# Log-sum-exp of 16,384 rows: another split of the loads and rows between three engines, and another middle range check

## The chip, the core and the metric

The kernel runs on one core of a Trainium2 chip. The metric is the device time of one execution in microseconds (us); the median of three runs is given. The core's engines have separate instruction queues and meet only at semaphores: TensorE (PE), VectorE (DVE), ScalarE (ACT), GpSimd (POOL) and SyncE (SP), which here issues all loads and stores to one DMA queue that 16 DMA engines serve.

## The reference

```
x: (32, 512, 1024) float32
max_x = max(x, axis=-1)
out   = max_x + log(sum(exp(x - max_x), axis=-1))        # (32, 512) float32
```

Each of the 32 x 512 = 16,384 rows of 1024 numbers gives one number.

## The kernel before

The rows are spread over 128 partitions, 128 rows to each. The first 112 rows of a partition (W = 112) come from one part of x, the last 16 from another, so that the results can be stored in two pieces. From here on "a row" is one row of 1024 elements on every partition at once.

The kernel leaves out the subtraction of the maximum: it sums exp(x) directly and takes the logarithm. At the end a range check looks whether all sums lie between 1e-15 and 1e15; if one does not, a second, safe pass runs (everything under `nc.If`). With these inputs it is skipped.

The work is written out by hand in the table LOADS. Each entry is one DMA load: its size in rows and what is done with it. A load goes into `ring`, which holds 48 rows; a load that does not fit at the end starts again at the front. SP issues the loads in order, and each waits (function `load`) until the rows that it overwrites have been summed. For each part of an entry ACT computes one exponential over the part's rows in place (L213), and the letters say who sums them:

- R n: DVE sums n rows with one reduction (L224).
- G n: POOL adds the second half of each of n rows to the first (L219, "folds"), later DVE sums the halves with one reduction (`sum_folded`, L148). That sum comes at the end of the load's entry, or where H or C stands.
- T n: DVE takes n rows one by one by halves: one operation adds the halves and accumulates the sum (`add_halves`, L156); a small read of the accumulator follows each.
- a, b: the two pieces of the last row, 256 and 768 elements. DVE takes a by halves, ACT sums b while it exponentiates it (L208).
- C: the middle range check over the sums so far. L: the early Ln of the first 112 sums (L199), whose store (L245) follows.

Several letters joined by + share one exponential. A part's exponential may reach beyond its last row, to the end of the load; the rest of that row comes with the next load. So an engine's order is the order of the table, and what one engine has not finished can hold up the others only through the semaphores: ACT waits for landings, DVE and POOL for ACT, DVE for POOL, SP for the sums that free the ring.

The range check (`check`, L163 to L174) is, for a group of sums: one operation with two inputs that counts in `bad` the sums below 1e-15 (L163), a reduction that gives their `total` (L167), and two small matmuls that add both into `count`. It is called once at C and once at the end. After the last sum the end is: ACT's Ln of sums 112 to 126 (L249), which waits for DVE's last sum; the Ln of the last row (L251), whose two pieces meet there; the store (L255); beside it the second check, the comparison (L263) and the branch. Ahead of the sixteenth load's pieces `addr_align(128)` (L186) puts padding into DVE's instructions up to a boundary.

Of the kernel before, what the change touches and what calls it, by code (L numbers as in the profile page):

```python
# [9 lines left out]
LOW, HIGH = 1e-15, 1e15  # L10
# [7 lines left out]

LOADS = [
# [4 lines left out]
]  # L26


# [23 lines left out]
def kernel(  # L52
# [5 lines left out]
    nc = tc.nc  # L58
# [7 lines left out]
    AF = mybir.ActivationFunctionType  # L66
    AX = mybir.AxisListType
    ALU = mybir.AluOpType

    x_flat = x.flatten_outer_dims()  # L70
    n, d = x_flat.shape
    assert n % P == 0
    NC = n // P
    H = d // 2
    W = NC - B
    LAST = NC - 1
# [6 lines left out]
    def source(e0, size):  # L83
# [6 lines left out]
        ])  # L90
        for size, parts in LOADS
    ]
    assert sum(size for size, _ in loads) == NC * d

    def sbuf(name, cols, dtype=fp32, rows=P):
        return nc.alloc_sbuf_tensor(name, [rows, cols], dtype).ap()

    ring = sbuf("ring", RING * d)
    sumexp = sbuf("sumexp", NC + 1)
    res = sbuf("res", NC)  # L100
    clamped = sbuf("clamped", NC)
    bad = sbuf("bad", 2)
    total = sbuf("total", 2)
    far = sbuf("far", 1)
    ones = sbuf("ones", 1)
    fine = sbuf("fine", 1, i32, 1)
    count = nc.alloc_psum_tensor("count", [1, 1], fp32).ap()

    landed = [nc.alloc_semaphore(f"landed{i}") for i in range(len(loads))]
    act = Counted(nc, nc.scalar, "act")  # L110
    dve = Counted(nc, nc.vector, "dve")
    pe = Counted(nc, nc.tensor, "pe")
    pool = Counted(nc, nc.gpsimd, "pool")
# [8 lines left out]
    constants = pool.did(nc.gpsimd.memset(far, 100 * HIGH))  # L122


    users = []

    def load(i, here, done_before, size):
        for a, b, who, at in users:
            if a < here + size and b > here:
                sp.wait(who, at)  # L130
        users[:] = [u for u in users if not (u[0] < here + size and u[1] > here)]
        return nc.sync.dma_start(
            out=ring[:, here : here + size], in_=source(done_before, size)
        ).then_inc(landed[i], 16)

    c = 0
    p = 0
    here = 0
    done_before = 0
    first_load = None  # L140
    folded = []
    summed = []

    def sum_folded():
        for c0, p0, s, at in folded:
            dve.wait(pool, at)
            half = ring[:, p0 : p0 + s * d].rearrange("p (c d) -> p c d", d=d)[:, :, 0:H]
            at = dve.did(nc.vector.reduce_sum(out=sumexp[:, c0 : c0 + s], in_=half, axis=AX.X))  # L148
            users.append((p0, p0 + s * d, dve, at))
            summed.append((c0, c0 + s, at))  # L150
        folded.clear()

    def add_halves(v, col):
        h = v.shape[-1] // 2
        lo = v[:, 0:h]
        return dve.did(nc.vector.scalar_tensor_tensor(  # L156
            out=lo, in0=lo, scalar=1.0, in1=v[:, h : 2 * h],
            op0=ALU.mult, op1=ALU.add, accum_out=sumexp[:, col : col + 1],
        ))

    def check(k, c0, c1):
        dve.wait(dve, dve.n)
        dve.did(nc.vector.scalar_tensor_tensor(  # L163
            out=clamped[:, c0:c1], in0=sumexp[:, c0:c1], scalar=LOW, in1=sumexp[:, c0:c1],
            op0=ALU.max, op1=ALU.not_equal, accum_out=bad[:, k : k + 1],
        ))
        at = dve.did(nc.vector.reduce_sum(  # L167
            out=total[:, k : k + 1], in_=sumexp[:, c0:c1], axis=AX.X
        ))
        if k == 0:  # L170
            pe.wait(pool, constants)
        pe.wait(dve, at)
        pe.did(nc.tensor.matmul(count, lhsT=bad[:, k : k + 1], rhs=far, start=k == 0, stop=False))  # L173
        pe.did(nc.tensor.matmul(count, lhsT=ones, rhs=total[:, k : k + 1], start=False, stop=False))  # L174

    for i, (size, parts) in enumerate(loads):
        if here + size > RING * d:
            assert here == p
            p = here = 0
        dma = load(i, here, done_before, size)  # L180
        first_load = first_load or dma.ins
        end = here + size
        done_before += size
        act.wait(landed[i], 16)
        if i == ALIGNED:
            nc.vector.addr_align(128)  # L186
        for k, part in enumerate(parts):
            if part[0][0] == "H":
                sum_folded()
                continue  # L190
            if part[0][0] == "C":
                sum_folded()
                checked = c
                check(0, 0, c)
                continue
            if part[0][0] == "L":
                assert c >= W
                act.wait(dve, max(at for c0, _, at in summed if c0 < W))
                ln_early = act.did(nc.scalar.activation(  # L199
                    out=res[:, 0:W], in_=sumexp[:, 0:W], func=AF.Ln  # L200
                ))
                continue
            rows = sum(s for how, s in part if how in "RTG")
            more = any(q[0][0] not in "HLC" for q in parts[k + 1 :])
            upto = p + rows * d if more else end
            v = ring[:, here:upto]
            if part[-1][0] == "b":
                last = act.did(nc.scalar.activation(  # L208
                    out=v, in_=v, func=AF.Exp, accum_out=sumexp[:, NC : NC + 1]
                ))  # L210
                here = upto
                continue
            at = act.did(nc.scalar.activation(out=v, in_=v, func=AF.Exp))  # L213
            here = upto
            for how, s in part:
                rows = ring[:, p : p + s * d].rearrange("p (c d) -> p c d", d=d)
                if how == "G":
                    pool.wait(act, at)
                    folded.append((c, p, s, pool.did(nc.gpsimd.tensor_tensor(  # L219
                        out=rows[:, :, 0:H], in0=rows[:, :, 0:H], in1=rows[:, :, H:d], op=ALU.add,  # L220
                    ))))
                elif how == "R":
                    dve.wait(act, at)
                    users.append((p, p + s * d, dve, dve.did(nc.vector.reduce_sum(  # L224
                        out=sumexp[:, c : c + s], in_=rows, axis=AX.X
                    ))))
                    summed.append((c, c + s, dve.n))
                elif how == "T":
                    dve.wait(act, at)
                    for r in range(s):  # L230
                        n_sums = add_halves(rows[:, r, :], c + r)
                        users.append((p + r * d, p + (r + 1) * d, dve, n_sums))
                        summed.append((c + r, c + r + 1, n_sums))
                elif how == "a":
                    dve.wait(act, at)
                    summed.append((LAST, NC, add_halves(ring[:, p:upto], LAST)))
                    s = 0
                c += s
                p += s * d
        sum_folded()  # L240
        assert here == end
    assert c == LAST
    assert sorted(q for c0, c1, _ in summed for q in range(c0, c1)) == list(range(NC))
    sp.wait(act, ln_early)
    nc.sync.dma_start(out=out_rows, in_=res[:, 0:W]).then_inc(sp.sem, 16)  # L245

    sums = dve.n
# [1 line left out]
    act.did(nc.scalar.activation(out=res[:, W:LAST], in_=sumexp[:, W:LAST], func=AF.Ln))  # L249
    act.wait(act, last)  # L250
    ln_last = act.did(nc.scalar.activation(  # L251
        out=res[:, LAST:NC], in_=sumexp[:, NC : NC + 1], func=AF.Ln, bias=sumexp[:, LAST:NC]
    ))
    sp.wait(act, ln_last)
    nc.sync.dma_start(out=out_rest, in_=res[:, W:NC]).then_inc(stored, 16)  # L255

    check(1, checked, NC)
    pe.wait(act, last)
    at = pe.did(nc.tensor.matmul(  # L259
        count, lhsT=ones, rhs=sumexp[:, NC : NC + 1], start=False, stop=True  # L260
    ))
    dve.wait(pe, at)
    at = dve.did(nc.vector.tensor_scalar(out=fine, in0=count, scalar1=HIGH, scalar2=None, op0=ALU.is_lt))  # L263
# [6 lines left out]
    with nc.If(all_fine < 1):  # L270
# [5 lines left out]
        for c0 in range(0, NC, RING):  # L276
            s = min(RING, NC - c0)
            v = ring[:, 0 : s * d].rearrange("p (c d) -> p c d", d=d)
# [4 lines left out]
            for c1, c2 in ((c0, edge), (edge, c0 + s)):  # L283
                if c1 == c2:
                    continue
                nc.scalar.dma_start(
                    out=ring[:, (c1 - c0) * d : (c2 - c0) * d],
                    in_=source(c1 * d, (c2 - c1) * d),
# [4 lines left out]
                out=neg, in_=v, op=ALU.max, axis=AX.X, negate=True  # L293
# [3 lines left out]
                out=v, in0=v, in1=neg[:, :, None].to_broadcast([P, s, d])  # L297
# [5 lines left out]
                out=sumexp[:, c0 : c0 + s], in_=v, axis=AX.X  # L303
# [71 lines left out]
```

## Time and profile before

| | |
|---|---|
| median of three runs | 162.37 us (162.37 to 162.44) |
| the profiled execution, its own time | 162.29 us |
| its span | 161.0 us |
| DVE, ACT, POOL, PE busy | 119.1, 115.0, 32.4, 0.5 us |
| DMA queue of the loads, share of 16 engines | 97.4% |
| read from HBM | 67.11 MB |

The span runs from the program's first instruction (the first load, at 0.00) to the last. Times in the timeline are us from its start. A timeline line gives start, duration, engine, line of the kernel, operation, what it writes and reads, the shape, and in brackets the idle time before it with what ended that. Runs of the same operation are merged (x3). An instruction may start while the one before it on the same engine is still shown: its fixed part overlaps. The chain of waits goes back from the last instruction, at each step to what released it. Groups by form give busy us, the mean ns of one, and the idle time before.

### The profile page before, as it was taken

What the parts mean: (1) busy time and instruction counts of PE and PEld (TensorE: products, weight loads), DVE (VectorE), ACT (ScalarE), POOL (GpSimd) and SP (SyncE); (2) the same over time, 40 slices, a digit from 0 to 9 for tenths busy, and PEclk for the clock granted to TensorE, in tenths of its full rate; (3) what the DMA queues carried; (4) which work ended last, traced back from release to release, by engine and by line L of the source; (5) the groups of instructions that cost most, each with busy time, mean ns of one, the idle gap of its engine ahead of it and who ended that gap; (6) DMA issues with size and microseconds to landing.
All of it is one profiled execution on the core that took longest, in us unless ns stands there. A gap on an engine that the chain in (4) does not pass through costs nothing.

```text
span 161.0 us, 202 instructions
## 1 busy us (share of the span) xinstructions
PE 0.5 (0%) x10; PEld 0.3 (0%) x10; DVE 119.1 (74%) x48; ACT 115.0 (71%) x32; POOL 32.4 (20%) x15
## 2 busy tenths in 40 slices
PE   0000000000000000000000000000000000000000
PEld 0000000000000000000000000000000000000000
DVE  0000000019999499995999999999999999999996
ACT  3000059980799609994199938996997999799995
POOL 0000000000000000000008800006950806737700
DMA  7996996996996996996999969899997999999991
GB/s 261 521 521 261 521 521 261 521 521 261 521 521 261 521 521 261 521 521 261 495 469 469 469 294 507 378 401 469 455 455 336 448 420 450 390 435 412 425 409 33
DMA packets 2882, 67.18 MB, mean 417 GB/s; under 512 B 577, under 2 KB 577, under 8 KB 1345
## 3 DMA queue, kind: packets, MB, share of 16 engines
q1 hardware_dynamic: 2880, 67.18, 97.4%
q14 instruction: 2, 0.01, 0.0%
HBM read 67.11 MB, written 0.07 MB: 417 GB/s over the span
## 4 chain that ended last, share of the span: by engine, by line
DVE 52%; DMA 30%; ACT 12%; POOL 4%; issue 1%; DVEq 0%; PE 0%
DVE sumexp L224 38%; DMA ring<-in_x_dram 30%; ACT ring L213 12%; DVE sumexp L148 10%; POOL ring L219 4%; DVE ring L156 3%; DVE clamped L163 1%; DVEq L186 0%; DVE total L167 0%; PE count L173 0%; DVE fine L263 0%; PE count L259 0%; PE count L174 0%
## 5 line engine op out<-in xcount | busy, mean ns | idle before, releaser
L213 ACT ACTIVATE ring<-ring 128x16384 f32<-128x16384 f32 (+22 forms) x26 | 112.3, 4371 | 42.5 <-DMA ring<-in_x_dram 42.4
L224 DVE TENSOR_REDUCE sumexp<-ring 128x16 f32<-128x16384 f32 (+6 forms) x10 | 96.1, 9639 | 40.0 <-ACT ring L213 40.0
L219 POOL TENSOR_TENSOR ring<-ring 128x1024 f32<-128x1024 f32 (+5 forms) x9 | 32.1, 3579 | 118.3 <-ACT ring L213 118.3
L148 DVE TENSOR_REDUCE sumexp<-ring 128x2 f32<-128x1024 f32 (+5 forms) x9 | 16.1, 1802 | 0.4 <-POOL ring L219 0.4
L156 DVE SCALAR_TENSOR_TENSOR ring<-ring 128x512 f32<-128x512 f32 (+1 forms) x11 | 6.5, 642 | 0.0
L120 ACT ACT_TABLE_LOAD x1 | 1.3, 1283 | 1.4 <-PEq L61 1.4
L163 DVE SCALAR_TENSOR_TENSOR clamped<-sumexp 128x114 f32<-128x114 f32 (+1 forms) x2 | 0.9, 462 | 0.1
L208 ACT ACTIVATE ring<-ring 128x768 f32<-128x768 f32 x1 | 0.8, 843 | 0.1
L173 PE MATMUL count<-far,bad 128*1 128x1 f32 x4 | 0.4, 163 | 159.2 <-DVE total L167 159.2
L156 DVE DVE_READ_ACCUMULATOR ring<-ring 128x1 f32 x11 | 0.8, 76 | 0.0
L173 PEld LDWEIGHTS count<-far,bad 128*1 128x1 f32 x4 | 0.2, 80 | 159.2 <-POOL ring L219 151.1
L249 ACT ACTIVATE res<-sumexp 128x15 f32<-128x15 f32 x1 | 0.2, 216 | 0.4 <-DVE ring L156 0.4
L263 DVE TENSOR_SCALAR fine<-count 1x1 int32<-1x1 f32 x1 | 0.1, 147 | 0.4 <-PE count L259 0.4
L167 DVE TENSOR_REDUCE total<-sumexp 128x1 f32<-128x114 f32 (+1 forms) x2 | 0.4, 212 | 0.0
L174 PE MATMUL count<-total,ones 128*1 128x1 f32 x4 | 0.4, 163 | 0.0
L121 POOL MEMSET ones<- 128x1 f32 x1 | 0.1, 98 | 1.0 <-POOLq L61 1.0
L199 ACT ACTIVATE res<-sumexp 128x112 f32<-128x112 f32 x1 | 0.3, 280 | 0.0
L251 ACT ACTIVATE res<-sumexp 128x1 f32<-128x1 f32 x1 | 0.3, 279 | 0.0
L174 PEld LDWEIGHTS count<-total,ones 128*1 128x1 f32 x4 | 0.2, 81 | 0.0
L259 PE MATMUL count<-sumexp,ones 128*1 128x1 f32 x2 | 0.2, 163 | 0.0
L208 ACT ACTIVATION_READ_ACCUMULATOR ring<-ring 128x1 f32 x1 | 0.2, 186 | 0.0
L163 DVE DVE_READ_ACCUMULATOR clamped<-sumexp 128x1 f32 x2 | 0.2, 79 | 0.0
(6 smaller groups left out, 0.6 us busy)
## 6 DMA issues: line engine op xcount, KB each, us to landing
ring<-in_x_dram SPq DMA_DIRECT2D x1, 7376.0 KB, 24.9
ring<-in_x_dram SPq DMA_DIRECT2D x1, 5936.0 KB, 19.6
ring<-in_x_dram SPq DMA_DIRECT2D x1, 4768.0 KB, 16.4
ring<-in_x_dram SPq DMA_DIRECT2D x1, 3520.0 KB, 15.1
ring<-in_x_dram SPq DMA_DIRECT2D x1, 2976.0 KB, 21.8
ring<-in_x_dram SPq DMA_DIRECT2D x1, 1792.0 KB, 27.4
ring<-in_x_dram SPq DMA_DIRECT2D x1, 1520.0 KB, 25.0
ring<-in_x_dram SPq DMA_DIRECT2D x1, 1360.0 KB, 19.2
```

The costliest lines, as they stand in the source:

```text
L120: nc.scalar.preload_act_table_set("natural_log_exp_and_others")
L148: at = dve.did(nc.vector.reduce_sum(out=sumexp[:, c0 : c0 + s], in_=half, axis=AX.X))
L156: return dve.did(nc.vector.scalar_tensor_tensor(out=lo, in0=lo, scalar=1.0, in1=v[:, h : 2 * h], op0=ALU.mult, op1=ALU.add, accum_out=sume ...
L163: dve.did(nc.vector.scalar_tensor_tensor(out=clamped[:, c0:c1], in0=sumexp[:, c0:c1], scalar=LOW, in1=sumexp[:, c0:c1], op0=ALU.max, op1=A ...
L167: at = dve.did(nc.vector.reduce_sum(out=total[:, k : k + 1], in_=sumexp[:, c0:c1], axis=AX.X))
L173: pe.did(nc.tensor.matmul(count, lhsT=bad[:, k : k + 1], rhs=far, start=k == 0, stop=False))
L174: pe.did(nc.tensor.matmul(count, lhsT=ones, rhs=total[:, k : k + 1], start=False, stop=False))
L199: ln_early = act.did(nc.scalar.activation(out=res[:, 0:W], in_=sumexp[:, 0:W], func=AF.Ln))
L208: last = act.did(nc.scalar.activation(out=v, in_=v, func=AF.Exp, accum_out=sumexp[:, NC : NC + 1]))
L213: at = act.did(nc.scalar.activation(out=v, in_=v, func=AF.Exp))
L219: folded.append((c, p, s, pool.did(nc.gpsimd.tensor_tensor(out=rows[:, :, 0:H], in0=rows[:, :, 0:H], in1=rows[:, :, H:d], op=ALU.add,))))
L224: users.append((p, p + s * d, dve, dve.did(nc.vector.reduce_sum(out=sumexp[:, c : c + s], in_=rows, axis=AX.X))))
```

## The change

The table is rewritten, with 17 loads for 18. The first three loads were summed in full by DVE; now POOL folds six rows of the second and five of the third. Six T rows (in the fifth and seventh loads) stand ahead of row 112. Two rows (A, in the ninth load) are exponentiated one by one by ACT with the sum taken at the same time. The exponentials of many parts are joined. The padding still stands ahead of the sixteenth load's pieces.

The middle check no longer counts and totals on its own. It takes the least and the total of the first 116 sums with two reductions into two spare columns right behind the sums (LEAST, TOTAL; the sum of b moves to a third, REST). The check at the end covers the sums from 116 on and these columns, and the two matmuls of the middle are gone. The early Ln waits for the middle check.

```
 LOADS = [
-    (16, "R16"), (16, "R16"), (16, "R16"), (16, "G6 H R10"), (14.40625, "R9 G5"),
-    (11.59375, "G3 R5 R4"), (9.3125, "G3 H R6"), (6.875, "G4 R3"), (5.8125, "G2 H R4"),
-    (2.96875, "G2 C"), (3.5, "G2 H T2"), (2.65625, "G1 T2 L"), (1.46875, "T1"),
-    (1.6875, "T2"), (1.28125, "T1"), (0.9375, "T1"), (0.75, "T1+a"), (0.75, "b"),
+    (16, "R16"), (16, "G6+R10"), (16, "R11+G5"), (16, "G4 R12"), (15.28125, "R8+G5 T2"),
+    (10.71875, "G6+R5"), (10.28125, "R2 G4 T4"), (5.75, "G2+R4"), (5.96875, "G3 A2 R1"),
+    (4.53125, "R3 G1 C"), (2.84375, "T3"), (2.59375, "R1+T1 L"), (2, "T2"),
+    (1.34375, "T2"), (1.125, "T1"), (0.8125, "T1+a"), (0.75, "b"),
 ]
...
+    LEAST, TOTAL, REST = NC, NC + 1, NC + 2
+    sumexp = sbuf("sumexp", NC + 3)
...
-    def check(k, c0, c1):
+    def check_early(c):
+        dve.wait(act, summed_by_act)
         dve.wait(dve, dve.n)
-        dve.did(nc.vector.scalar_tensor_tensor(
-            out=clamped[:, c0:c1], in0=sumexp[:, c0:c1], scalar=LOW, in1=sumexp[:, c0:c1],
-            op0=ALU.max, op1=ALU.not_equal, accum_out=bad[:, k : k + 1],
-        ))
-        at = dve.did(nc.vector.reduce_sum(
-            out=total[:, k : k + 1], in_=sumexp[:, c0:c1], axis=AX.X
-        ))
...
+        for op, col in ((ALU.min, LEAST), (ALU.add, TOTAL)):
+            at = dve.did(nc.vector.tensor_reduce(
+                out=sumexp[:, col : col + 1], in_=sumexp[:, 0:c], op=op, axis=AX.X
+            ))
+        return at
...
+            if part[0][0] == "A":
+                assert here == p
+                for _ in range(part[0][1]):
+                    v = ring[:, p : p + d]
+                    summed_by_act = act.did(nc.scalar.activation(
+                        out=v, in_=v, func=AF.Exp, accum_out=sumexp[:, c : c + 1]
+                    ))
+                    users.append((p, p + d, act, summed_by_act))
...
-    check(1, checked, NC)
+    dve.wait(act, summed_by_act)
+    dve.wait(dve, sums)
+    dve.did(nc.vector.scalar_tensor_tensor(
+        out=clamped[:, 0 : LEAST + 1 - checked], in0=sumexp[:, checked : LEAST + 1], scalar=LOW,
+        in1=sumexp[:, checked : LEAST + 1], op0=ALU.max, op1=ALU.not_equal, accum_out=bad,
+    ))
+    at = dve.did(nc.vector.reduce_sum(
+        out=total, in_=sumexp[:, checked : TOTAL + 1], axis=AX.X
+    ))
```

More of the change, by code (lines that the diff above doesn't have):

```diff
@@ L98 @@
     ring = sbuf("ring", RING * d)
-    sumexp = sbuf("sumexp", NC + 1)
+    LEAST, TOTAL, REST = NC, NC + 1, NC + 2
+    sumexp = sbuf("sumexp", NC + 3)
     res = sbuf("res", NC)
     clamped = sbuf("clamped", NC)
-    bad = sbuf("bad", 2)
-    total = sbuf("total", 2)
+    bad = sbuf("bad", 1)
+    total = sbuf("total", 1)
     far = sbuf("far", 1)
@@ L142 @@
     summed = []
+    summed_by_act = 0
+    by_act = 0
     def sum_folded():
@@ L159, in add_halves @@
         ))
-    def check(k, c0, c1):
+    def check_early(c):
+        dve.wait(act, summed_by_act)
         dve.wait(dve, dve.n)
-        dve.did(nc.vector.scalar_tensor_tensor(
-            out=clamped[:, c0:c1], in0=sumexp[:, c0:c1], scalar=LOW, in1=sumexp[:, c0:c1],
-            op0=ALU.max, op1=ALU.not_equal, accum_out=bad[:, k : k + 1],
-        ))
-        at = dve.did(nc.vector.reduce_sum(
-            out=total[:, k : k + 1], in_=sumexp[:, c0:c1], axis=AX.X
-        ))
[L170 to L174, printed above, removed]
+        for op, col in ((ALU.min, LEAST), (ALU.add, TOTAL)):
[3 more added lines that the diff above has]
+        return at
     for i, (size, parts) in enumerate(loads):
@@ L193 @@
                 checked = c
-                check(0, 0, c)
+                all_checked = check_early(c)
                 continue
@@ L197 @@
                 assert c >= W
-                act.wait(dve, max(at for c0, _, at in summed if c0 < W))
+                assert checked >= W
+                act.wait(dve, all_checked)
                 ln_early = act.did(nc.scalar.activation(
@@ L201 @@
                 ))
+                continue
+            if part[0][0] == "A":
[6 more added lines that the diff above has]
+                    users.append((p, p + d, act, summed_by_act))
+                    by_act += 1
+                    c += 1
+                    p += d
+                    here += d
                 continue
@@ L208 @@
                 last = act.did(nc.scalar.activation(
-                    out=v, in_=v, func=AF.Exp, accum_out=sumexp[:, NC : NC + 1]
+                    out=v, in_=v, func=AF.Exp, accum_out=sumexp[:, REST : REST + 1]
                 ))
@@ L242 @@
     assert c == LAST
-    assert sorted(q for c0, c1, _ in summed for q in range(c0, c1)) == list(range(NC))
+    assert by_act + sum(c1 - c0 for c0, c1, _ in summed) == NC
     sp.wait(act, ln_early)
@@ L251 @@
     ln_last = act.did(nc.scalar.activation(
-        out=res[:, LAST:NC], in_=sumexp[:, NC : NC + 1], func=AF.Ln, bias=sumexp[:, LAST:NC]
+        out=res[:, LAST:NC], in_=sumexp[:, REST : REST + 1], func=AF.Ln, bias=sumexp[:, LAST:NC]
     ))
@@ L255 @@
     nc.sync.dma_start(out=out_rest, in_=res[:, W:NC]).then_inc(stored, 16)
-    check(1, checked, NC)
+    dve.wait(act, summed_by_act)
[7 more added lines that the diff above has]
+    ))
+    pe.wait(pool, constants)
+    pe.wait(dve, at)
+    pe.did(nc.tensor.matmul(count, lhsT=bad, rhs=far, start=True, stop=False))
+    pe.did(nc.tensor.matmul(count, lhsT=ones, rhs=total, start=False, stop=False))
     pe.wait(act, last)
     at = pe.did(nc.tensor.matmul(
-        count, lhsT=ones, rhs=sumexp[:, NC : NC + 1], start=False, stop=True
+        count, lhsT=ones, rhs=sumexp[:, REST : REST + 1], start=False, stop=True
     ))
```

## The prediction

> **What bounds the kernel now.** I read the page first (shares, queues), then the chain of waits from its end backwards, then the timeline of the last 30 us, because the page's shares average over stages with different limits.
>
> ```profile
> span 161.0 us, 202 instructions
> ...
> PE 0.5 (0%) x10; PEld 0.3 (0%) x10; DVE 119.1 (74%) x48; ACT 115.0 (71%) x32; POOL 32.4 (20%) x15
> ...
> q1 hardware_dynamic: 2880, 67.18, 97.4%
> ```
>
> The load queue keeps the 16 DMA engines busy for 97.4% of the span. No edit to the compute engines can beat that; what is left is the few tenths between the last bytes and the last store. The chain says who owns them:
>
> ```profile
> 0.00 21.78 DMA ring<-in_x_dram
> ...
> 92.02 3.35 DVE sumexp L148
> 95.37 20.39 DVE sumexp L224 x2
> ...
> 118.48 9.72 DVE sumexp L224 x2
> ...
> 128.20 3.32 DVE sumexp L148 x2
> ...
> 152.12 2.44 DVE ring L156 x8
> ...
> 159.07 0.18 DVE clamped L163 x2
> ```
>
> From 92.02 on everything is VectorE (DVE). It also gives the prices. 19 rows (19,456 elements) in two reductions take 20.39, 9 rows 9.72, two reductions of 1,536 take 3.32: elements / 0.96 per ns plus 0.06 us each. A row by halves (T) is 2.44 / 4 = 0.61. The end, in the timeline:
>
> ```profile
> 151.61 0.28 ACT L199 ACTIVATE res<-sumexp 128x112 f32<-128x112 f32 x1
> 151.80 5.84 ACT L213 ACTIVATE ring<-ring 128x1504 f32<-128x1504 f32 x5
> ...
> 157.75 0.84 ACT L208 ACTIVATE ring<-ring 128x768 f32<-128x768 f32 x1
> ...
> 158.50 0.19 ACT L208 ACTIVATION_READ_ACCUMULATOR ring<-ring 128x1 f32 x1
> ...
> 158.75 0.28 DVE L156 SCALAR_TENSOR_TENSOR ring<-ring 128x128 f32<-128x128 f32 x1
> ...
> 159.07 0.22 ACT L249 ACTIVATE res<-sumexp 128x15 f32<-128x15 f32 x1 [0.39 <-DVE ring L156]
> 159.07 0.17 DVE L163 SCALAR_TENSOR_TENSOR clamped<-sumexp 128x14 f32<-128x14 f32 x1
> ...
> 159.19 0.28 ACT L251 ACTIVATE res<-sumexp 128x1 f32<-128x1 f32 x1
> ...
> 159.50 0.34 SPq L255 DMA_DIRECT2D out_dram<-res  x1
> ```
>
> and, among the DMA issues with KB and us to landing:
>
> ```profile
> out_dram<-res SPq DMA_DIRECT2D x1, 8.0 KB, 1.4
> ```
>
> ScalarE (ACT) finished its own last sum at 158.50 + 0.19 = 158.69 and then idled until 159.07 for DVE's last sum. The store at 159.50 lands 1.4 later, which is the end of the span. So I forecast one instant, the start of the Ln at L249 (159.07 now); all after it keeps its distance. ACT's pace is here too: the 112-element Ln shows 0.28, yet the next instruction starts 0.19 after it, so an activation occupies elements / 1.2 per ns plus 0.093, and its result comes 0.09 later. The profiled execution took 162.29, 1.3 around its span of 161.0; the median of the three timed runs is 162.37, so I carry the difference over to that.
>
> **Landings.** Summing the load table: 64 rows in the first four loads of both versions, 90 in the first six, 112 in the first nine. These loads land when they do now, as long as the queue never runs dry:
>
> ```profile
> 79.85 13.95 ACT L213 ACTIVATE ring<-ring 128x6144 f32<-128x6144 f32 x2 [5.48 <-DMA ring<-in_x_dram]
> ...
> 97.26 12.59 ACT L213 ACTIVATE ring<-ring 128x9216 f32<-128x9216 f32 x2 [3.46 <-DMA ring<-in_x_dram]
> 106.19 0.33 SPq L132 DMA_DIRECT2D ring<-in_x_dram  x1
> ...
> 111.28 10.28 ACT L213 ACTIVATE ring<-ring 128x2656 f32<-128x2656 f32 x3 [1.43 <-DMA ring<-in_x_dram]
> ...
> 138.01 13.70 ACT L213 ACTIVATE ring<-ring 128x1856 f32<-128x1856 f32 x7 [0.91 <-DMA ring<-in_x_dram]
> ```
>
> 79.85 to 111.28 is 26 rows, 1.209 a row. The fifth load (0.875 row longer) is ready at 97.26 + 1.06 = 98.32, the seventh (10.28 rows) at 111.28 + 12.43 = 123.71, the ninth at 138.01. The last lands now just ahead of 157.75. The 16 rows after 138.01 take 19.74 in nine loads; at 1.205 a row for the large loads that is 0.05 per extra load, and one load is dropped: ready at 157.70.
>
> **VectorE's own work.** Longer forms are scaled from these rows (and the reverse for shorter):
>
> ```profile
> L213 ACT ACTIVATE ring<-ring 128x10240 f32<-128x10240 f32 x1 | 8.7, 8720 | 0.0
> ...
> L213 ACT ACTIVATE ring<-ring 128x4096 f32<-128x4096 f32 x2 | 7.2, 3601 | 0.0
> ...
> L219 POOL TENSOR_TENSOR ring<-ring 128x3072 f32<-128x3072 f32 x1 | 6.7, 6735 | 83.7 <-ACT ring L213 83.7
> ...
> L219 POOL TENSOR_TENSOR ring<-ring 128x2048 f32<-128x2048 f32 x1 | 4.5, 4537 | 5.5 <-ACT ring L213 5.5
> ...
> L219 POOL TENSOR_TENSOR ring<-ring 128x512 f32<-128x512 f32 x1 | 1.3, 1317 | 0.0
> ```
>
> The new early splits (G6, G5, G4 beside DVE) fall where DVE waits for data anyway; what they buy is that DVE has no backlog left at 109.6. There: fifth load, 13,312 elements, 8.72 + 2.56 = 11.28, done 109.60; then 2,336 elements, ACT free at 111.55; then the sixth load's 10,976, 9.33, done 120.88. GpSimd (POOL) starts its six rows 0.07 later and needs 6.74: 127.69. DVE meanwhile: 8 rows from 109.62 (8.60), T2 (1.22), five folded (2.73), five (5.39): free at 127.56. So the sum of the six folded rows starts at 127.71. From there to the last piece "a": ten reductions of 19,456 elements, 20.27 + 0.60 = 20.87; 14 rows T, 8.57; the middle check. (Over the whole kernel DVE sums 73 rows in full, 36 folded and 16 as T, before 89, 28 and 10; two rows, A, become ACT's.)
>
> The middle check:
>
> ```profile
> 145.97 5.95 POOL L219 TENSOR_TENSOR ring<-ring 128x1024 f32<-128x1024 f32 x3 [3.77 <-ACT ring L213]
> ...
> 148.81 1.21 DVE L148 TENSOR_REDUCE sumexp<-ring 128x2 f32<-128x1024 f32 x1
> ...
> 150.05 0.75 DVE L163 SCALAR_TENSOR_TENSOR clamped<-sumexp 128x114 f32<-128x114 f32 x1
> ...
> 150.73 0.26 DVE L167 TENSOR_REDUCE total<-sumexp 128x1 f32<-128x114 f32 x1
> 150.91 1.20 DVE L148 TENSOR_REDUCE sumexp<-ring 128x2 f32<-128x1024 f32 x1
> ```
>
> Now it costs 0.11 (148.81 to 150.05 against 1.13 for this reduction elsewhere) + 0.68 + 0.18. The 0.68 is odd: the 14-element form takes 0.17, and 100 more elements are 0.10. POOL explains it: its last fold (1.32) ended at 151.92, so the one before ended near 150.6, inside those 0.75. The operation with two inputs waited for POOL; the one-input reduction beside the next fold (150.73) took its plain 0.26. The new check is two such reductions: 0.11 + 0.18 + 0.18 = 0.48 (0.2 to 0.7 at the ends). But T rows have two inputs too. T4 of the seventh load is due at 127.71 + 3.27 + 2.19 = 133.17, while POOL folds G4 (exponentials done at 123.71 + 1.82 + 3.60 = 129.13, POOL until 133.74): the first T waits 0.57. The other T rows find POOL idle.
>
> The Trainium skill, "SBUF — State Buffer", section Who interferes with whom, states this rule: a DVE instruction with two SBUF inputs contends with a GpSimd instruction that reads SBUF, and the second to issue blocks until the first ends. The 0.75 row agrees. It speaks against moving T rows in front of row 112; without it the T4 wait would be 0 and the DVE sum below 0.57 less.
>
> Sum: 127.71 + 20.87 + 8.57 + 0.48 + 0.57 = 158.20 for "a", and L249 came 0.32 after "a" (158.75 to 159.07): **158.52**.
>
> **ScalarE.** From 138.01 it has no pause: seventh and eighth loads (14.08 from 123.71) end at 137.8. To the last b: 12 exponentials and the Ln, as now, over 21,728 elements: 18.11 + 12 x 0.093 + 0.02 + 0.19 = 19.44. New are two read-outs for the A rows. The only such row (158.50, 0.19) has nothing queued behind it, so what it costs the next instruction lies between 0 and 0.19. An activation hides half of its fixed 0.19 from the next; I take 0.09 each, so ACT is free for b at 138.01 + 19.44 + 0.18 = 157.63. The piece before b carries "T1+a": result 157.72, DVE 0.02 later, T 0.61, "a", 0.32: **158.67**. At 0.19 each: 158.87.
>
> **The last load.** b starts at 157.70, its sum 0.94 later: **158.64**.
>
> Forecast: the latest, 158.67, is 0.40 before 159.07: 161.89 in the profiled execution, **161.97** in the median. Three chains end within 0.15, so b's landing is the floor: 161.94.
>
> Costed at nothing: the two PE pairs (PE is idle); the early store, issued about 1 us later but behind all loads in its queue either way; the final check, same size, beside ACT's last Ln. Also the padding ahead of the last pieces:
>
> ```profile
> L186 DVEq NOP  x19: 18/18/18, 156.0 to 156.9; - x19
> ```
>
> DVE's sequencer runs it while DVE is busy. Some 14 more instructions (with read-outs) stand ahead of it, so about 5 remain; past the boundary it could be 100 more at 0.05, 5 us.
>
> **Rivals.**
>
> Read-outs in full: the ACT chain ends at 158.87, 0.20 before now: **162.17**. For it: the 0.19 row itself. Against it: activations overlap by half.
>
> Late load, the one that ends slower. The seventh load overwrites the fourth's place, whose 12 rows now come in one piece: exponentials until 83.36 + 10.43 = 93.79, reduction until 106.68, four folded rows until 108.96. It is issued at 109.0, 2.26 before the sixth has landed at 111.26. Now the shortest lead is 5.1 (issue 106.19), without a gap. A queue that starts empty needs 21.78 - 19.34 = 2.43 beyond a load's own time, so a gap of 0.17 is the nearest estimate, giving L249 at 158.84, **162.14**; ends 0 and 2.8. A gap shifts all three chains. From 0.40 on nothing is gained; from 0.73 it is slower by over 0.2%; midway, 1.4, **163.4**. Against it: the 2.43 is the price of an empty queue, and here the sixth load's packets still run when the order goes out.
>
> Not as it says: POOL blocks more T rows than reckoned, or a fold meets a T. One more wait of 0.57 puts DVE at 159.09: no change, **162.39**.
>
> **How the numbers follow.** Chances: forecast with the floor 0.52; read-outs 0.17; short gap 0.12; blocked T rows 0.09; long gap or long padding 0.10. 0.2%, about what a measurement of this kernel can tell from no change, is 0.32. Faster by more: the first, and a bit of the next two, 0.55. Within: 0.35. Slower: 0.10. The range goes from the floor less the spread of the runs (0.07) to read-outs and gap together (158.87 + 0.17 = 159.04, 162.34): 161.86 to 162.36.
>
> **What would show it.** Right: L249 at 158.6 to 158.9 with no idle time or under 0.2 before it; "a" near 158.35; ACT without a pause from 138.0; its A rows 1.03 apart; T4's first piece 1.2 long near 133.2; two reductions of about 0.26 near 150.6; fifth to ninth loads ready at 98.3, 111.3, 123.7, 130.7 and 138.0. Wrong: the seventh or any later load late by more than 0.2; A rows 1.13 apart; DVE waiting for POOL in the last 20 us; b ready after 157.8.

## The result, and the profile after

The changed kernel is slower: 164.31 us in the median of four runs (163.73 to 164.96), the kernel before 162.39 beside it; ratio 1.0119, 95% interval 1.0081 to 1.0157. Its runs lie over a range of 1.2 us, those of before over 0.07. The profiled execution took 164.29.

From the page of the changed kernel: the head, the engines, the load queue and the chain that ended last.

```profile
span 163.0 us, 192 instructions
...
PE 0.3 (0%) x6; PEld 0.2 (0%) x6; DVE 110.7 (68%) x60; ACT 114.5 (70%) x32; POOL 41.1 (25%) x15
...
q1 hardware_dynamic: 2736, 67.18, 96.6%
...
DMA 55%; ACT 26%; DVE 16%; issue 1%; SPq 0%; PE 0%; DVEq 0%
```

DVE lost 8.4 us of work, and the span grew by 2. The load queue's share fell from 97.4% to 96.6%, and the chain, which ran over DVE for 52% of the span before, now runs over the DMA for 55%. Where the DMA took over, the chain in order of time shows (start, duration, what):

```profile
98.51 11.31 ACT ring L227
109.81 0.02 issue
109.84 8.70 DVE sumexp L238
118.53 0.02 issue
118.55 0.33 SPq L136
118.88 0.04 issue
118.92 21.43 DMA ring<-in_x_dram
140.35 0.02 issue
140.38 2.74 ACT ring L227
...
161.06 0.18 DVE clamped L273 x2
```

From 140.38 to 157 the chain is ACT behind a load that landed at 140.35. The forecast had that load, the ninth, at 138.0. The chain leads back to the orders at 118.55, but these only queued behind what was late already, so they are not the cause. The step at which it became late is in the timeline of the changed kernel:

```profile
109.25 0.33 SPq L136 DMA_DIRECT2D ring<-in_x_dram  x1
...
126.09 17.02 ACT L227 ACTIVATE ring<-ring 128x2048 f32<-128x2048 f32 x5 [5.01 <-DMA ring<-in_x_dram]
...
160.00 0.84 ACT L222 ACTIVATE ring<-ring 128x768 f32<-128x768 f32 x1
...
160.74 0.28 DVE L162 SCALAR_TENSOR_TENSOR ring<-ring 128x128 f32<-128x128 f32 x1
...
161.06 0.21 ACT L263 ACTIVATE res<-sumexp 128x15 f32<-128x15 f32 x1
...
161.49 0.34 SPq L269 DMA_DIRECT2D out_dram<-res  x1
```

The seventh load was ordered at 109.25 and ready at 126.09, not 123.71. Everything behind it is late by about as much: b starts at 160.00 instead of 157.70. From the trace's landing events: the sixth load landed at 111.46, so the order came 2.21 ahead of it; by its size the seventh should follow 12.43 later, at 123.89, and its last part came at 126.07, 2.18 late.

How it was late shows in the DMA's busy share in 40 slices between 109 and 119, first of the kernel before, then of the changed one:

```profile
DMA  9000099900099000799000999003990007990009
```

```profile
DMA  9840009790990994409999478499973999973779
```

A load is spread over the 16 DMA engines. The records of their packets appear where they start: before, the engines go in step, all starting a packet within two or three slices (a slice is 0.25 us), none in the next ones. In the changed kernel the step is lost from about 110.5 on, where the seventh load begins. By the packet records the first packets of its 16 parts start between 110.53 and 112.51 and take 1.56 to 2.35 us each. The trace's 16 landing events of that load lie between 123.80 and 126.07, a spread of 2.27 (0.67 for the load before it), and every later load keeps a spread of 2.1 to 2.3. A load has landed when its slowest part has, so ACT waits for the slowest engine from there to the end.

### The profile page after: what moved, and what is told of

Same layout as the page of the kernel before. It is cut to its first block, busy times and chain, and to the rows that moved or that the text cites. A ratio compares the mean times of both kernels' runs of the same rounds, so it can differ in the third digit from the quotient of the medians.

```text
span 163.0 us, 192 instructions
## 1 busy us (share of the span) xinstructions
PE 0.3 (0%) x6; PEld 0.2 (0%) x6; DVE 110.7 (68%) x60; ACT 114.5 (70%) x32; POOL 41.1 (25%) x15
## 3 DMA queue, kind: packets, MB, share of 16 engines
q1 hardware_dynamic: 2736, 67.18, 96.6%
## 4 chain that ended last, share of the span: by engine, by line
DMA 55%; ACT 26%; DVE 16%; issue 1%; SPq 0%; PE 0%; DVEq 0%
DMA ring<-in_x_dram 55%; ACT ring L227 24%; DVE sumexp L238 12%; DVE ring L162 2%; DVE sumexp L154 2%; ACT ring L208 1%; SPq L136 0%; PE count L282 0%; ACT res L200 0%; DVE clamped L273 0%; DVE fine L289 0%; DVE total L277 0%; PE count L285 0%; DVEq L186 0%; PE count L283 0%
## 5 line engine op out<-in xcount | busy, mean ns | idle before, releaser
L227 ACT ACTIVATE ring<-ring 128x16384 f32<-128x16384 f32 (+17 forms) x22 | 109.9, 5050 | 45.4 <-DMA ring<-in_x_dram 45.3
L238 DVE TENSOR_REDUCE sumexp<-ring 128x1 f32<-128x1024 f32 (+9 forms) x11 | 79.5, 7227 | 48.8 <-ACT ring L227 48.8
L233 POOL TENSOR_TENSOR ring<-ring 128x3072 f32<-128x3072 f32 (+5 forms) x9 | 40.8, 4529 | 109.2 <-ACT ring L227 109.2
L154 DVE TENSOR_REDUCE sumexp<-ring 128x6 f32<-128x3072 f32 (+5 forms) x9 | 20.5, 2278 | 0.0
L162 DVE SCALAR_TENSOR_TENSOR ring<-ring 128x512 f32<-128x512 f32 (+1 forms) x17 | 11.1, 703 | 1.9 <-ACT ring L227 1.9
L208 ACT ACTIVATE ring<-ring 128x1024 f32<-128x1024 f32 x2 | 2.1, 1040 | 0.0
L162 DVE DVE_READ_ACCUMULATOR ring<-ring 128x1 f32 x17 | 1.4, 81 | 0.0
L171 DVE TENSOR_REDUCE sumexp<-sumexp 128x1 f32<-128x116 f32 x2 | 0.5, 269 | 0.0
L263 ACT ACTIVATE res<-sumexp 128x15 f32<-128x15 f32 x1 | 0.2, 214 | 0.1
```

What stands on the lines that cost most here:

```text
L162: return dve.did(nc.vector.scalar_tensor_tensor(out=lo, in0=lo, scalar=1.0, in1=v[:, h : 2 * h], op0=ALU.mult, op1=ALU.add, accum_out=sume ...
L171: at = dve.did(nc.vector.tensor_reduce(out=sumexp[:, col : col + 1], in_=sumexp[:, 0:c], op=op, axis=AX.X))
L208: summed_by_act = act.did(nc.scalar.activation(out=v, in_=v, func=AF.Exp, accum_out=sumexp[:, c : c + 1]))
L233: folded.append((c, p, s, pool.did(nc.gpsimd.tensor_tensor(out=rows[:, :, 0:H], in0=rows[:, :, 0:H], in1=rows[:, :, H:d], op=ALU.add,))))
```

## The experiments

**Theory A**: the seventh load is ordered too late, the engines start it one by one, and the slowest then sets each landing. **Theory B**: the new table slows the transfers all along. **Theory C**: the rows by halves or ScalarE's own sums are what is late.

**An earlier order.** The four folded rows of the fourth load are summed ahead of its twelve full rows:

```
-    (16, "R16"), (16, "G6+R10"), (16, "R11+G5"), (16, "G4 R12"), (15.28125, "R8+G5 T2"),
+    (16, "R16"), (16, "G6+R10"), (16, "R11+G5"), (16, "G4 H R12"), (15.28125, "R8+G5 T2"),
```

> The changed kernel with one letter more, H behind G4 in the fourth load: DVE sums the four folded rows before the twelve full rows instead of after them, so the seventh load is ordered at about 107.2 instead of 109.2, some 4.3 us ahead of the sixth load's landing (2.2 in the changed kernel). Theory A (late order: the 16 DMA engines start the seventh load one by one, and the slowest sets every later landing): if 4.3 is lead enough the seventh load is ready at 123.9 again, b at 157.9, the kernel takes 161.9 to 162.1; if not, a smaller part of the 2.2 us remains. Theory B (the DMA is slowed by something that the new table does all along: more folds by GpSimd, the joined exponentials): nothing of that is touched, 164.3. Theory C (the rows by halves or ScalarE's sums are what is late): nothing touched either, 164.3.

Measured: 161.91 (161.83 to 162.17, 11 runs), ratio to before 0.9977, interval 0.9968 to 0.9986. Its timeline:

```profile
106.84 0.33 SPq L136 DMA_DIRECT2D ring<-in_x_dram  x1
...
123.69 5.42 ACT L227 ACTIVATE ring<-ring 128x2048 f32<-128x2048 f32 x2 [2.83 <-DMA ring<-in_x_dram]
...
157.74 0.84 ACT L222 ACTIVATE ring<-ring 128x768 f32<-128x768 f32 x1
158.49 0.19 ACT L222 ACTIVATION_READ_ACCUMULATOR ring<-ring 128x1 f32 x1
158.60 0.22 ACT L263 ACTIVATE res<-sumexp 128x15 f32<-128x15 f32 x1
```

and its DMA share between 109 and 119, in step again:

```profile
DMA  9000099900079900039900039900009990009990
```

The first packets of the seventh load now start between 110.33 and 110.83 and take 1.56 us each. One letter takes away the whole loss, and nothing of B or C was touched. Both fall. The kernel now does what the prediction said of the change.

**Still earlier.** The same with the twelve rows in two pieces ("G4 H R6 R6").

> As the run with H behind G4, and the twelve rows of the fourth load in two pieces of six, so that DVE begins on them some 5 us earlier and the seventh load is ordered at about 104.3, 7.1 us ahead of the sixth landing. Theory A: no gap; ready at 123.9, b at 157.9, 161.9 to 162.1. Theories B and C: 164.3 as before.

Measured: 162.11 (162.04 to 162.28), ratio 0.9986 (0.9977 to 0.9995). The order came 7.04 ahead, the load in time: more lead than 4.4 brings nothing. That it is 0.2 above the run before is not explained; this version has one exponential more, and so have the next two, which are as far above it.

**Half of it.** "G2 H G2 R12": two folded rows summed ahead, two behind.

> The changed kernel with the fourth load's four folded rows in two pairs, the first summed ahead of the twelve full rows and the second behind: the seventh load is ordered at about 108.2, a lead of 3.2 us. Theory A: a part of the loss, 1.1 us if the loss falls one for one with the lead (163.2), and a spread of about 1.6 us between the first and the last of the 16 landings of the seventh load. Theories B and C: 164.3.

Measured: 162.13 (162.03 to 162.31), ratio 0.9987 (0.9978 to 0.9996); ordered at 108.14, 3.17 ahead, ready in time, spread 0.60. The expected partial loss of 1.1 is not there: the loss does not fall one for one with the lead.

**Close to the edge.** "G1 H G3 R12".

> The changed kernel with one of the fourth load's four folded rows summed ahead of the twelve full rows and three behind: the seventh load is ordered at about 108.7, a lead of 2.7 us, between the 2.2 that cost 2.2 us and the 3.2 that cost nothing. If the price is that of a queue that starts empty (2.43 in the prediction): 162.1, the 16 parts of the seventh load within 0.7 us of each other. If a lead just short of enough is what throws the engines out of step: something of the loss and its scatter stays, 162.5 to 164.

Measured: 162.20, ratio 1.0003 (0.9980 to 1.0026); eleven of twelve runs lie between 162.06 and 162.35, one at 164.46. In the profiled one the order came at 108.76, 2.62 ahead, and the load in time; one of the 16 first packets took 1.71 us instead of 1.56. So 2.6 us is probably close to the edge. That the odd run fell over it is likely but not shown, as that run has no profile.

**The same fault in the old table.** One wait in `load` of the kernel before:

```
+        if i == 6:
+            sp.wait(act, 7)
```

> The kernel before with one wait added: SP orders the seventh load only when ScalarE has ended the fifth load's last exponential, at about 109.9 instead of 106.2, a lead of 1.4 us instead of 5.1. Nothing else moves. Theory A: the same loss appears in the old table, 3.0 us at the seventh landing (2.2 plus the 0.8 of lead that is shorter still), 164.5 to 165.2 and scattered runs. Theories B and C: the old table has neither the folds nor the rows by halves, and the queue still holds the sixth load when the order comes: 162.4, or 162.8 if only the time from the order to the first packet (1.0) is missing.

Measured: 163.82 (163.50 to 163.99), ratio 1.0082 (1.0068 to 1.0096). The order came at 109.97, 1.30 ahead; the seventh load was 1.54 late, spread 0.95. The loss appears without folds, rows by halves or sums by ScalarE: A again. Its size is not the expected 3.0.

**Later in the new table.** The version with H, with `sp.wait(act, 6)` at the same place:

> The version with H, and one wait more: the seventh load is ordered only when ScalarE has ended the exponential of the fifth load's thirteen rows, at about 109.9, a lead of 1.4 us (2.2 in the changed kernel). If the loss falls one for one with the lead, it is 0.8 more than in the changed kernel: 165.1. If the old table's loss at 1.3 us (1.5 at the landing, spread 0.95) is the rule for an order that comes so late that all engines start afresh together, the loss is 1.0 to 1.6 and smaller than at 2.2: 163.0 to 163.6, and the runs scatter less than those of the changed kernel.

Measured: 164.15 (164.05 to 164.36), ratio 1.0113 (1.0098 to 1.0127). Ordered at 109.77, 1.56 ahead; 2.06 late, spread 1.67. With less lead than the changed kernel it loses no more, and the loss lies between the two that were expected; only the smaller scatter came as expected. By the packets, 14 of the engines ended the load about 1.1 late, the other two 0.6 and 1.2 after the last of these.

**Surely too late.** `sp.wait(act, 7)` instead:

> As the run with the seventh load's order held until about 109.9, but held until ScalarE has also ended the fifth load's two remaining rows, at about 111.7: 0.3 us after the sixth load has landed, a lead of -0.3 us instead of 1.6. The queue is then surely empty. If from a lead of about 2.6 downwards the loss grew one for one, and the stragglers are a cost on top that every late order pays once: 1.9 more than at 1.6 us, 166.0. If the loss is a fixed price of an interrupted queue: 164.2, as at 1.6.

Measured: 164.71 (164.69 to 164.82), ratio 1.0144 (1.0126 to 1.0162). Neither expectation holds. The order and the DMA share between 109 and 119:

```profile
111.94 0.33 SPq L138 DMA_DIRECT2D ring<-in_x_dram  x1
```

```profile
DMA  9400000000000009994000039900039900009930
```

No packet of the seventh load starts before 112.89, 0.95 after the order. The first 16 start within 0.7 us and take 1.78 to 2.46 us each, not 1.56; from the second on the engines go in step, and the spread is 0.41. The load is ready at 126.62, which is 2.25 beyond order and own time: close to the 2.43 that the first load of the kernel before gave. All together, with one profiled execution to each row and the median of the timed runs beside it (the lead is the sixth load's landing less the order of the seventh):

| version | lead of the order, us | seventh load late by | spread of its 16 parts | median |
|---|---|---|---|---|
| H, two pieces | 7.04 | 0.0 | 0.62 | 162.11 |
| H | 4.40 | 0.0 | 0.53 | 161.91 |
| two and two | 3.17 | 0.0 | 0.60 | 162.13 |
| one and three | 2.62 | 0.0 | 0.52 | 162.20 |
| the change | 2.21 | 2.18 | 2.27 | 164.31 |
| H and a wait | 1.56 | 2.06 | 1.67 | 164.15 |
| old table and a wait | 1.30 | 1.54 | 0.95 | 163.82 |
| H and a later wait | -0.49 | 2.74 | 0.41 | 164.71 |

With 2.25 to 2.43 as the need of an empty queue, a lead of 2.21 should cost 0.0 to 0.2, 1.56 0.7 to 0.9 and 1.30 1.0 to 1.1. What is on top, 0.4 to 2.1, comes in these runs only where the order is given before the load ahead has landed, and it comes as spread: some engines are thrown out of step. In all four late versions the first packets are slow as well: 1.88, 2.21 and 2.14 us in the mean for the three with the new table, where 1.56 is usual, and 2.06 for 1.41 in the old one. Why the first packets are slow, and why the engines lose their step when the order is late but not when it is later still, these runs do not show.

**The new check alone.** The old table with the code of the change:

> The kernel before with its old table and only the new range check (two one-input reductions in the middle instead of the two-input operation that waited for GpSimd). Theory from the prediction: the wait of about 0.3 us is gone, DVE's last sum and the Ln at L249 come 0.25 earlier, 162.1 (ratio 0.9985). Rival: the sum of two folded rows behind the check has to wait for the same fold of GpSimd and takes the gain back: 162.36.

Measured: 162.30 (162.16 to 162.42), ratio 0.9996, interval 0.9987 to 1.0005: unclear. The median is 0.07 lower where 0.27 was forecast. Its timeline shows part of the reason:

```profile
148.97 1.22 DVE L154 TENSOR_REDUCE sumexp<-ring 128x2 f32<-128x1024 f32 x1
150.22 0.45 DVE L171 TENSOR_REDUCE sumexp<-sumexp 128x1 f32<-128x114 f32 x2
150.86 1.22 DVE L154 TENSOR_REDUCE sumexp<-ring 128x2 f32<-128x1024 f32 x1 [0.19 <-POOL ring L233]
...
159.11 0.21 ACT L263 ACTIVATE res<-sumexp 128x15 f32<-128x15 f32 x1 [0.23 <-DVE ring L162]
```

The check no longer waits for POOL, but the sum behind it needs the same fold and waits 0.19 itself, so a part of the wait was only moved. What is left: from the sum ahead of the check to the sum behind it, 1.89 us pass instead of 2.10 (148.81 to 150.91 before), and to the Ln 10.14 instead of 10.26. So 0.12 of the forecast 0.25 reaches the end, and since this execution is 0.16 later than that of before already at the sum ahead of the check, the Ln is not earlier by the clock. The rival is right in part.

**T rows beside a fold.** H, and the seventh load as "G4 R2 T4" instead of "R2 G4 T4":

> The version with H and the seventh load's first two parts exchanged (G4 R2 T4), so that GpSimd's four folds are over before DVE comes to the rows by halves: the first of these takes 0.68 instead of 1.4. DVE has 0.6 to 0.7 us less to do on its way to the end. Theory from the prediction: ScalarE's chain and the last load end at the same instant, so nothing is gained: 161.9, within 0.1 of the version with H. Rival: DVE still sets the end, 161.7 or lower if the last load allows it.

Measured: 161.87 (161.80 to 161.96), ratio 0.9968 (0.9955 to 0.9981), 0.04 below H, which the runs can't tell from H: the lowest median of all versions. The first of the four rows by halves, with the fold beside it (H):

```profile
129.18 4.54 POOL L233 TENSOR_TENSOR ring<-ring 128x2048 f32<-128x2048 f32 x1 [1.55 <-ACT ring L227]
...
133.13 1.15 DVE L162 SCALAR_TENSOR_TENSOR ring<-ring 128x512 f32<-128x512 f32 x1
...
134.21 0.68 DVE L162 SCALAR_TENSOR_TENSOR ring<-ring 128x512 f32<-128x512 f32 x1
```

and without ("G4 R2 T4"):

```profile
133.24 0.68 DVE L162 SCALAR_TENSOR_TENSOR ring<-ring 128x512 f32<-128x512 f32 x1
```

POOL ends at 133.72, and the row's result comes 0.56 later: it waited 0.47. Without the wait nothing to speak of is gained, since the other two chains end at the same time.

**Without ScalarE's sums.** H, and "G3 T2 R1" for "G3 A2 R1" in the ninth load:

> The version with H, and the two rows that ScalarE summed itself (A2, ninth load) given to DVE by halves (T2) while GpSimd folds the three rows of the same load. DVE gets 1.2 us of work and a wait for the fold on top. Theory from the prediction, that DVE's own sum ends only some 0.1 to 0.2 us ahead of the other two chains: DVE now sets the end, 1.2 to 1.6 us later, 163.1 to 163.5. Rival, that DVE has slack: 162.

Measured: 163.35 (163.27 to 163.66), ratio 1.0065 (1.0047 to 1.0083), 1.44 above H. ACT's last Ln then waits for DVE:

```profile
160.13 0.21 ACT L263 ACTIVATE res<-sumexp 128x15 f32<-128x15 f32 x1 [1.38 <-DVE ring L162]
```

DVE has no slack: the two sums by ScalarE are what lets it keep up with the loads.

## Why the prediction was wrong

**The step that failed** is the rival "late load". The forecast let the loads land as before "as long as the queue never runs dry"; the rival saw that the seventh load is ordered 2.26 ahead of the sixth landing (2.21 measured) and where from (twelve rows in one piece, four folded behind them). It then priced that lead with the start of an empty queue, 2.43, so a gap of 0.17 (with ends at 0 and 2.8), and gave the short gap a chance of 0.12 and a long one 0.10 together with the padding. The gap was 2.18 at the landing, and it cost 2.40 in the time (164.31 against 161.91 with H). The term that was mis-sized is this gap, and the form behind it was wrong: an empty queue needs about what the rival said (2.25), but a lead of 2.21 and less costs 1.5 to 2.7 us at once and not the lead that is missing. What the prediction held against the rival, that the sixth load's packets still run when the order goes out, is the case in which the engines lost their step. The trace of before had only shown that 5.1 is enough; no row of it showed what a lead of 2.26 costs. The runs put the smallest lead that is enough between 2.21 and 3.17, probably near 2.6. Why a lead that is short by so little costs so much stays open.

**What held**, measured on the version with H, where the load is in time:

- The forecast without a gap: 161.97; measured 161.91. The Ln at L249 was forecast for 158.67; it came at 158.60 (L263 there).
- The landings of the fifth to ninth loads: 98.3, 111.3, 123.7, 130.7 and 138.0 forecast; 98.26, 111.24, 123.67, 130.63 and 137.87 in the trace.
- "a" near 158.35: 158.27. The middle check 0.48: the two reductions with the wait are 150.46 to 150.83, and 0.12 ahead, 0.49.
- The read-outs at 0.09: ACT's two A rows and the next exponential start 1.04 apart.

```profile
140.54 1.04 ACT L208 ACTIVATE ring<-ring 128x1024 f32<-128x1024 f32 x1
...
141.58 1.04 ACT L208 ACTIVATE ring<-ring 128x1024 f32<-128x1024 f32 x1
...
142.62 9.94 ACT L227 ACTIVATE ring<-ring 128x1024 f32<-128x1024 f32 x5
```

- The wait of T4 for POOL: 0.57 forecast, 0.47 measured. The rule of the Trainium skill ("SBUF — State Buffer", Who interferes with whom) that was weighed there is borne out in both directions, with the fold beside it and without.
- The padding: about 5 expected, 5 in the changed kernel.

```profile
L186 DVEq NOP  x5: 18/18/18, 159.3 to 159.6; - x5
```

- Three chains that end within 0.15: taking work off DVE ("G4 R2 T4") brings 0.04, giving it 1.2 us and a wait costs 1.44.

The rivals "read-outs in full" and "blocked T rows" did not come about.

## What to carry to other kernels

In a kernel that lives on one DMA queue, work out for every load the lead of its order over the landing before it, from the instruction that frees its buffer; an edit that makes that instruction longer, or puts another one ahead of it, moves the order. Keep the lead well above the smallest one that some version has shown to be enough in all its runs (here 3.2 us): a lead of 2.62 was in time in the profiled run, one of 2.21 cost 2 us, and the loss stayed to the end, since nothing in this kernel has slack. If such an edit is otherwise good, reorder the freeing sum first: one letter turned 1.2% slower into 0.2% faster.

## What the runs showed that was not expected

- A lead that is 0.4 us under one that was in time (2.62) cost nearly as much as one that is 3 us under it: 2.18 late at a lead of 2.21, 2.74 at -0.49.
- Out-of-step DMA engines did not come back into step: in the changed kernel the spread of the 16 parts stayed at 2.1 to 2.3 from the seventh load to the last.
- An order into an empty queue had its first packet 0.95 us later (111.94 to 112.89) and landed 2.25 us beyond the load's own time.
